# Sum of squared differences: several rows per load packet, float32 differences in place, a last row in five shrinking chunk pairs, and a seeded last sum

## The chip, the cores and the metric

The kernel runs on one core of a Trainium2 chip. The metric is the device time of one execution in microseconds (us). The profile's span is about 1.8 us shorter than that time. Runs of one kernel on one chip mostly agree within 0.3%; single runs lie further out.

## The reference

```python
batch, dim = 1024, 4096
x, y: float32 [1024, 4096]
out = np.sum((x - y) ** 2, axis=-1)        # float32 [1024]
```

The two inputs are 33.55 MB, the output 4 KB. Every element is read once, subtracted once and squared once.

## The kernel before

Partition p holds the rows 8p to 8p + 7, one of them per step i. VectorE subtracts into a bfloat16 tile, and ScalarE squares and sums it (its output goes to a dummy tile in PSUM, the sum to one column of `results`). The rows 6 and 7 are cut into chunks, so that work can begin before a whole row is there. Some chunks are squared on VectorE instead ("DD"), by an operation that multiplies and sums at once. In the trace that operation is CUSTOM_DVE_ANT_0 with a short READ_ACCUMULATOR after it.

```python
w6 = [2258, 1838];                 s6 = ["DA", "DD"]
w7 = [1467, 1316, 619, 308, 386];  s7 = ["DA", "DA", "DA", "DD", "DD"]

for i in range(ntiles - 2):                       # rows 0..5, data pool with 2 buffers
    xt, yt = data.tile([P, D], float32), data.tile([P, D], float32)
    dt = data.tile([P, D], bfloat16)
    nc.sync.dma_start(out=xt, in_=x[i:B:ntiles, :])
    nc.sync.dma_start(out=yt, in_=y[i:B:ntiles, :])
    nc.vector.tensor_sub(out=dt, in0=xt, in1=yt)
    nc.scalar.activation(out=junk, in_=dt, func=Square, accum_out=results[:, i : i + 1])
# ... loads of all chunks of rows 6 and 7 (cut) ...
emit_compute(w6, s6, ...)                         # per chunk: subtraction, then square-sum on ACT or DVE
nc.vector.tensor_reduce(out=results[:, i6 : i6 + 1], in_=part6, ...)
emit_compute(w7, s7, ...)
nc.vector.tensor_reduce(out=results[:, i7 : i7 + 1], in_=part7, ...)
nc.sync.dma_start(out=out, in_=results)
```

Of the kernel before, what the change touches and what calls it, by code (L numbers as in the profile page):

```python
# [1 line left out]
_os.environ.setdefault("NEURON_RT_ULTRASERVER_MODE", "4")  # L2

# [1 line left out]

# [4 lines left out]


@with_exitstack
def kernel(
    ctx: ExitStack,
    tc: tile.TileContext,
    x: bass.AP,
    y: bass.AP,
    axis: bass.AP,
    out: bass.AP,
):  # L20
    nc = tc.nc
    P = nc.NUM_PARTITIONS

    B, D = x.shape
    ntiles = (B + P - 1) // P

    data = ctx.enter_context(tc.tile_pool(name="data", bufs=2))
    chunkp = ctx.enter_context(tc.tile_pool(name="chunk", bufs=1))
    res = ctx.enter_context(tc.tile_pool(name="res", bufs=1))
    junkp = ctx.enter_context(tc.tile_pool(name="junkp", bufs=1, space=bass.MemoryType.PSUM))  # L30

    w6 = [2258, 1838]
    s6 = ["DA", "DD"]
    w7 = [1467, 1316, 619, 308, 386]
    s7 = ["DA", "DA", "DA", "DD", "DD"]
    assert sum(w6) == D and sum(w7) == D
    K6 = len(w6)
    K7 = len(w7)

    results = res.tile([P, ntiles], mybir.dt.float32)  # L40
    part6 = res.tile([P, K6], mybir.dt.float32)
    part7 = res.tile([P, K7], mybir.dt.float32)
    junk = junkp.tile([P, D], mybir.dt.float32)

    Square = mybir.ActivationFunctionType.Square
    i6 = ntiles - 2
    i7 = ntiles - 1

    xts = []
    yts = []  # L50
    dts = []
    for i in range(ntiles - 2):
        xt = data.tile([P, D], mybir.dt.float32, name="xt")
        yt = data.tile([P, D], mybir.dt.float32, name="yt")
        dt = data.tile([P, D], mybir.dt.bfloat16, name="dt")
        nc.sync.dma_start(out=xt, in_=x[i:B:ntiles, :])  # L56
        nc.sync.dma_start(out=yt, in_=y[i:B:ntiles, :])  # L57
        xts.append(xt)
        yts.append(yt)
        dts.append(dt)  # L60

        nc.vector.tensor_sub(out=dt, in0=xt, in1=yt)  # L62
        nc.scalar.activation(  # L63
            out=junk,
            in_=dt,
            func=Square,
            accum_out=results[:, i : i + 1],
        )

    def emit_chunks(tid, widths, strats, part):  # L70
        cxs, cys, cds, sqs = [], [], [], []
        c0 = 0
        for k, w in enumerate(widths):
            cx = chunkp.tile([P, w], mybir.dt.float32, name=f"cx{tid}_{k}")
            cy = chunkp.tile([P, w], mybir.dt.float32, name=f"cy{tid}_{k}")
            cd = chunkp.tile([P, w], mybir.dt.bfloat16, name=f"cd{tid}_{k}")
            nc.sync.dma_start(out=cx, in_=x[tid:B:ntiles, c0 : c0 + w])  # L77
            nc.sync.dma_start(out=cy, in_=y[tid:B:ntiles, c0 : c0 + w])
            sq = None
            if strats[k] == "DD":  # L80
                sq = chunkp.tile([P, w], mybir.dt.bfloat16, name=f"sq{tid}_{k}")
            cxs.append(cx)
            cys.append(cy)
            cds.append(cd)
            sqs.append(sq)
            c0 += w
        return cxs, cys, cds, sqs

    cx6, cy6, cd6, sq6 = emit_chunks(i6, w6, s6, part6)
    cx7, cy7, cd7, sq7 = emit_chunks(i7, w7, s7, part7)  # L90

    def emit_compute(widths, strats, cxs, cys, cds, sqs, part):
        for k, w in enumerate(widths):
            nc.vector.tensor_sub(out=cds[k], in0=cxs[k], in1=cys[k])  # L94
            if strats[k] == "DA":
                nc.scalar.activation(  # L96
                    out=junk[:, 0:w],
                    in_=cds[k],
                    func=Square,
                    accum_out=part[:, k : k + 1],  # L100
                )
            else:
                nc.vector.tensor_tensor_reduce(  # L103
                    out=sqs[k],
                    in0=cds[k],
                    in1=cds[k],
                    scale=1.0,
                    scalar=0.0,
                    op0=mybir.AluOpType.mult,
                    op1=mybir.AluOpType.add,  # L110
                    accum_out=part[:, k : k + 1],
                )

    emit_compute(w6, s6, cx6, cy6, cd6, sq6, part6)
    nc.vector.tensor_reduce(  # L115
        out=results[:, i6 : i6 + 1],
        in_=part6,
        axis=mybir.AxisListType.X,
        op=mybir.AluOpType.add,
    )  # L120
    emit_compute(w7, s7, cx7, cy7, cd7, sq7, part7)
    nc.vector.tensor_reduce(  # L122
        out=results[:, i7 : i7 + 1],
        in_=part7,
        axis=mybir.AxisListType.X,
        op=mybir.AluOpType.add,
    )

    nc.sync.dma_start(out=out, in_=results)


# [1 line left out]
_INS = ['x', 'y', 'axis']  # L133
_OUTS = [((1024,), 'float32')]
#: Inputs that are plain numbers.
_NUMBERS = {'axis': -1}


# [26 lines left out]
```

## Time and profile before

| what | before |
|---|---|
| time, median | 87.84 us (87.72 to 87.92) |
| span | 86.0 us |
| DMA packets | 3888 |
| one full pair of rows (4 MiB), landing to landing | 9.79 us, 428 GB/s |
| VectorE and ScalarE busy | 39.6 us and 29.4 us |
| store issued | 83.65 us |

VectorE and ScalarE are busy for less than half of the span, and the chain of waits on the page, shown in the prediction, is 78% DMA: the kernel waits for its loads. A read of the profile therefore splits into the start until the first bytes flow, the stream of loads, and the tail from the last landings to the store. (A load lands when its data are in; the wait for it ends then.) The span ends some 2.35 us after the store is issued.

### The profile page before, as it was taken

Reading aid. Unit: us, or ns where it says so; the run is one execution under the profiler, and the core shown is the slowest. Engines: PE = TensorE matmul, PEld = TensorE weight load, DVE = VectorE, ACT = ScalarE, POOL = GpSimd, SP = SyncE. Lnnn points to the kernel's source line nnn. Section 1 sums busy time; section 2 is a strip of 40 time slices with the busy share of each in tenths; the row PEclk is TensorE's granted clock in tenths of the full one; section 3 lists DMA queues with packets and bytes.
Section 4 is the critical chain, followed back from the end, with each engine's and each line's share of the span. In section 5 each row is a group of like instructions: output and inputs, shape, how many; then the busy total and the mean of one; then the engine's idle time right before and its main releaser. Section 6 shows DMA issues by size and latency. Waiting matters only on the chain.

```text
span 86.0 us, 143 instructions
## 1 busy us (share of the span) xinstructions
DVE 39.6 (46%) x21; ACT 29.4 (34%) x21; POOL 0.2 (0%) x4
## 2 busy tenths in 40 slices
DVE  0000009900496008910397007930198655996980
ACT  5000000098003940079002950069000996007630
POOL 0000000000000000000000000000000000000000
DMA  4799999999999999999999999999999999999900
GB/s 107 320 427 442 412 465 389 473 396 465 404 450 404 457 396 457 404 450 412 442 419 435 427 427 435 419 442 412 408 420 411 424 418 416 408 416 390 314 0 2
DMA packets 3888, 33.56 MB, mean 390 GB/s; under 512 B 560, under 2 KB 1072, under 8 KB 2096
## 3 DMA queue, kind: packets, MB, share of 16 engines
q1 hardware_dynamic: 3888, 33.56, 93.5%
HBM read 33.55 MB, written 0.00 MB: 390 GB/s over the span
## 4 chain that ended last, share of the span: by engine, by line
DMA 78%; DVE 14%; SPq 3%; issue 1%; DVEq 0%
DMA yt<-in_y_dram 41%; DMA cy<-in_y_dram 37%; DVE dt L62 10%; DVE cd L94 2%; SPq L56 2%; DVE sq L103 1%; SPq L57 1%; SPq L77 1%; DVE results L122 0%; DVEq L62 0%; DVEq L94 0%; DVEq L122 0%; DVE part L103 0%
## 5 line engine op out<-in xcount | busy, mean ns | idle before, releaser
L62 DVE TENSOR_TENSOR dt<-xt,yt 128x4096 bf16<-128x4096 f32 x6 | 26.6, 4425 | 39.8 <-DMA yt<-in_y_dram 39.8
L63 ACT ACTIVATE junk<-dt 128x4096 f32<-128x4096 bf16 x6 | 21.5, 3587 | 45.9 <-DVE dt L62 45.9
L94 DVE TENSOR_TENSOR cd<-cx,cy 128x2258 bf16<-128x2258 f32 (+6 forms) x7 | 9.7, 1379 | 3.9 <-DMA cy<-in_y_dram 3.8
L96 ACT ACTIVATE junk<-cd 128x2258 f32<-128x2258 bf16 (+3 forms) x4 | 5.4, 1354 | 6.5 <-DVE cd L94 6.4
L103 DVE CUSTOM_DVE_ANT_0 sq<-cd 128x1838 bf16<-128x1838 bf16 (+2 forms) x3 | 3.1, 1038 | 0.1
L63 ACT ACT_TABLE_LOAD x1 | 1.3, 1283 | 0.7 <-PEq L146 0.7
L63 ACT ACTIVATION_READ_ACCUMULATOR junk<-dt 128x1 f32 x6 | 1.1, 186 | 0.0
L96 ACT ACTIVATION_READ_ACCUMULATOR junk<-cd 128x1 f32 x4 | 0.7, 186 | 0.0
L103 DVE DVE_READ_ACCUMULATOR2_ANT part<- 128x1 f32 x3 | 0.2, 83 | 0.0
L122 DVE TENSOR_REDUCE results<-part 128x1 f32<-128x5 f32 x1 | 0.2, 159 | 0.1
L115 DVE TENSOR_REDUCE results<-part 128x1 f32<-128x2 f32 x1 | 0.2, 155 | 0.1
L146 POOL MEMSET const-bfloat16-1.0<- 128x1 bf16 x1 | 0.1, 102 | 0.0
L146 POOL MEMSET const-uint8-127<- 128x1 uint8 x1 | 0.1, 102 | 0.0
L146 POOL MEMSET const-float32-1.0<- 128x1 f32 x1 | 0.1, 99 | 0.0
L146 POOL MEMSET const-float32-0.0<- 128x1 f32 x1 | 0.1, 98 | 0.2 <-issue 0.2
## 6 DMA issues: line engine op xcount, KB each, us to landing
xt<-in_x_dram SPq DMA_DIRECT2D x6, 2048.0 KB, 10.1
yt<-in_y_dram SPq DMA_DIRECT2D x6, 2048.0 KB, 14.6
cx<-in_x_dram SPq DMA_DIRECT2D x1, 1129.0 KB, 16.9
cy<-in_y_dram SPq DMA_DIRECT2D x1, 1129.0 KB, 19.2
cx<-in_x_dram SPq DMA_DIRECT2D x1, 919.0 KB, 20.9
cy<-in_y_dram SPq DMA_DIRECT2D x1, 919.0 KB, 22.7
cx<-in_x_dram SPq DMA_DIRECT2D x1, 733.5 KB, 24.0
cy<-in_y_dram SPq DMA_DIRECT2D x1, 733.5 KB, 23.3
```

The lines of the kernel that those rows point to most:

```text
L56: nc.sync.dma_start(out=xt, in_=x[i:B:ntiles, :])
L57: nc.sync.dma_start(out=yt, in_=y[i:B:ntiles, :])
L62: nc.vector.tensor_sub(out=dt, in0=xt, in1=yt)
L63: nc.scalar.activation(out=junk, in_=dt, func=Square, accum_out=results[:, i : i + 1],)
L77: nc.sync.dma_start(out=cx, in_=x[tid:B:ntiles, c0 : c0 + w])
L94: nc.vector.tensor_sub(out=cds[k], in0=cxs[k], in1=cys[k])
L96: nc.scalar.activation(out=junk[:, 0:w], in_=cds[k], func=Square, accum_out=part[:, k : k + 1],)
L103: nc.vector.tensor_tensor_reduce(out=sqs[k], in0=cds[k], in1=cds[k], scale=1.0, scalar=0.0, op0=mybir.AluOpType.mult, op1=mybir.AluOpType.add,
L115: nc.vector.tensor_reduce(out=results[:, i6 : i6 + 1], in_=part6, axis=mybir.AxisListType.X, op=mybir.AluOpType.add,)
L122: nc.vector.tensor_reduce(out=results[:, i7 : i7 + 1], in_=part7, axis=mybir.AxisListType.X, op=mybir.AluOpType.add,)
L146: nc = _bacc.Bacc("TRN2", target_bir_lowering=False, num_devices=1)
```

## The change

Its intent is to spend fewer packets on the same bytes (a packet is the part of a load that goes to one partition; the trace has 128 of them per transfer and 16 more of 4 bytes, so 27 transfers make 3888): four rows of x in one load (64 KB per partition), then pairs of rows (32 KB). VectorE writes the float32 difference over x, so no tiles for differences are needed, and five large buffers fit: one of 64 KB per partition and four of 32 KB. Row 7 comes in five pairs that shrink. The last reduction is to move off the end: it runs before the last square-sum, and its result is the start value (the seed) of that sum. Row 6 is no longer cut.

```diff
-        nc.sync.dma_start(out=xt, in_=x[i:B:ntiles, :])         # per row, 16 KB per partition
-        nc.sync.dma_start(out=yt, in_=y[i:B:ntiles, :])
+    xv = x.rearrange("(p r) d -> p (r d)", p=P)
+    load(x03, xv, 0, 4 * D)                                     # 64 KB per partition
+    load(y01, yv, 0, 2 * D)                                     # 32 KB
+    load(y23, yv, 2 * D, 4 * D)
+    load(x45, xv, 4 * D, 6 * D)
+    load(y45, yv, 4 * D, 6 * D)
 ...
-        nc.vector.tensor_sub(out=dt, in0=xt, in1=yt)            # dt is bfloat16
+            nc.vector.tensor_sub(out=a, in0=a, in1=b)           # float32, over x
 ...
+    w7 = [1280, 1088, 768, 640, 320]
+    on_act = [True, False, True, True, False]
 ...
+        nc.vector.tensor_sub(out=a, in0=a, in1=b)
+        if k == K - 1:
+            nc.vector.tensor_reduce(out=head, in_=part, ...)    # parts 0..3
+        if on_act[k]:
+            square_sum(a, part[:, k : k + 1])
+        else:
+            nc.vector.tensor_tensor_reduce(
+                out=b, in0=a, in1=a, ...
+                scalar=head if k == K - 1 else 0.0,
+                accum_out=results[:, R - 1 : R] if k == K - 1 else part[:, k : k + 1],
+            )
```

More of the change, by code (lines that the diff above doesn't have):

```diff
@@ L22 @@
     P = nc.NUM_PARTITIONS
+    F32 = mybir.dt.float32
+    Square = mybir.ActivationFunctionType.Square
     B, D = x.shape
-    ntiles = (B + P - 1) // P
-    data = ctx.enter_context(tc.tile_pool(name="data", bufs=2))
-    chunkp = ctx.enter_context(tc.tile_pool(name="chunk", bufs=1))
+    R = B // P
+    xv = x.rearrange("(p r) d -> p (r d)", p=P)
+    yv = y.rearrange("(p r) d -> p (r d)", p=P)
+    ov = out.rearrange("(p r) -> p r", p=P)
+    wide = ctx.enter_context(tc.tile_pool(name="wide", bufs=1))
@@ L29 @@
+    pairs = ctx.enter_context(tc.tile_pool(name="pairs", bufs=1))
     res = ctx.enter_context(tc.tile_pool(name="res", bufs=1))
     junkp = ctx.enter_context(tc.tile_pool(name="junkp", bufs=1, space=bass.MemoryType.PSUM))
-    w6 = [2258, 1838]
-    s6 = ["DA", "DD"]
-    w7 = [1467, 1316, 619, 308, 386]
-    s7 = ["DA", "DA", "DA", "DD", "DD"]
-    assert sum(w6) == D and sum(w7) == D
-    K6 = len(w6)
-    K7 = len(w7)
-    results = res.tile([P, ntiles], mybir.dt.float32)
-    part6 = res.tile([P, K6], mybir.dt.float32)
@@ L42 @@
-    part7 = res.tile([P, K7], mybir.dt.float32)
-    junk = junkp.tile([P, D], mybir.dt.float32)
-    Square = mybir.ActivationFunctionType.Square
-    i6 = ntiles - 2
-    i7 = ntiles - 1
-    xts = []
-    yts = []
-    dts = []
-    for i in range(ntiles - 2):
-        xt = data.tile([P, D], mybir.dt.float32, name="xt")
-        yt = data.tile([P, D], mybir.dt.float32, name="yt")
-        dt = data.tile([P, D], mybir.dt.bfloat16, name="dt")
-        nc.sync.dma_start(out=xt, in_=x[i:B:ntiles, :])
-        nc.sync.dma_start(out=yt, in_=y[i:B:ntiles, :])
-        xts.append(xt)
-        yts.append(yt)
-        dts.append(dt)
-        nc.vector.tensor_sub(out=dt, in0=xt, in1=yt)
+    results = res.tile([P, R], F32)
@@ L63, with load, square_sum @@
+    junk = junkp.tile([P, D], F32)
+    w7 = [1280, 1088, 768, 640, 320]
+    on_act = [True, False, True, True, False]
+    assert sum(w7) == D
+    K = len(w7)
+    part = res.tile([P, K - 1], F32)
+    head = res.tile([P, 1], F32)
+    def load(dst, src, c0, c1):
+        nc.sync.dma_start(out=dst, in_=src[:, c0:c1])
+    def square_sum(d, acc):
         nc.scalar.activation(
-            out=junk,
-            in_=dt,
-            func=Square,
-            accum_out=results[:, i : i + 1],
-        )
@@ L70, in emit_chunks @@
-    def emit_chunks(tid, widths, strats, part):
-        cxs, cys, cds, sqs = [], [], [], []
-        c0 = 0
-        for k, w in enumerate(widths):
-            cx = chunkp.tile([P, w], mybir.dt.float32, name=f"cx{tid}_{k}")
-            cy = chunkp.tile([P, w], mybir.dt.float32, name=f"cy{tid}_{k}")
-            cd = chunkp.tile([P, w], mybir.dt.bfloat16, name=f"cd{tid}_{k}")
-            nc.sync.dma_start(out=cx, in_=x[tid:B:ntiles, c0 : c0 + w])
-            nc.sync.dma_start(out=cy, in_=y[tid:B:ntiles, c0 : c0 + w])
-            sq = None
-            if strats[k] == "DD":
-                sq = chunkp.tile([P, w], mybir.dt.bfloat16, name=f"sq{tid}_{k}")
-            cxs.append(cx)
-            cys.append(cy)
-            cds.append(cd)
-            sqs.append(sq)
-            c0 += w
-        return cxs, cys, cds, sqs
@@ L89 @@
-    cx6, cy6, cd6, sq6 = emit_chunks(i6, w6, s6, part6)
-    cx7, cy7, cd7, sq7 = emit_chunks(i7, w7, s7, part7)
-    def emit_compute(widths, strats, cxs, cys, cds, sqs, part):
-        for k, w in enumerate(widths):
-            nc.vector.tensor_sub(out=cds[k], in0=cxs[k], in1=cys[k])
-            if strats[k] == "DA":
-                nc.scalar.activation(
-                    out=junk[:, 0:w],
-                    in_=cds[k],
-                    func=Square,
-                    accum_out=part[:, k : k + 1],
-                )
-            else:
-                nc.vector.tensor_tensor_reduce(
-                    out=sqs[k],
-                    in0=cds[k],
-                    in1=cds[k],
-                    scale=1.0,
-                    scalar=0.0,
-                    op0=mybir.AluOpType.mult,
-                    op1=mybir.AluOpType.add,
-                    accum_out=part[:, k : k + 1],
-                )
@@ L114 @@
-    emit_compute(w6, s6, cx6, cy6, cd6, sq6, part6)
-    nc.vector.tensor_reduce(
-        out=results[:, i6 : i6 + 1],
-        in_=part6,
-        axis=mybir.AxisListType.X,
-        op=mybir.AluOpType.add,
-    )
-    emit_compute(w7, s7, cx7, cy7, cd7, sq7, part7)
-    nc.vector.tensor_reduce(
-        out=results[:, i7 : i7 + 1],
-        in_=part7,
-        axis=mybir.AxisListType.X,
-        op=mybir.AluOpType.add,
-    )
-    nc.sync.dma_start(out=out, in_=results)
+            out=junk[:, 0 : d.shape[1]], in_=d, func=Square, accum_out=acc
+        )
@@ new lines, in rows @@
+    def rows(xt, yt, n, r0):
+        for k in range(n):
+            a = xt[:, k * D : (k + 1) * D]
+            b = yt[:, k * D : (k + 1) * D]
+            nc.vector.tensor_sub(out=a, in0=a, in1=b)
+            square_sum(a, results[:, r0 + k : r0 + k + 1])
+    x03 = wide.tile([P, 4 * D], F32, name="wide_x", tag="wide_x")
+    y01 = pairs.tile([P, 2 * D], F32, name="ya", tag="ya")
+    y23 = pairs.tile([P, 2 * D], F32, name="yb", tag="yb")
+    x45 = pairs.tile([P, 2 * D], F32, name="xc", tag="xc")
@@ new lines @@
+    y45 = pairs.tile([P, 2 * D], F32, name="yc", tag="yc")
+    load(x03, xv, 0, 4 * D)
[3 more added lines that the diff above has]
+    load(y45, yv, 4 * D, 6 * D)
+    rows(x03[:, 0 : 2 * D], y01, 2, 0)
+    rows(x03[:, 2 * D : 4 * D], y23, 2, 2)
+    t6 = pairs.tile([P, 2 * D], F32, name="ya2", tag="ya")
+    t7 = pairs.tile([P, 2 * D], F32, name="yb2", tag="yb")
+    load(t6[:, 0:D], xv, 6 * D, 7 * D)
+    load(t6[:, D : 2 * D], yv, 6 * D, 7 * D)
@@ new lines @@
+    c0 = 0
+    for w in w7:
+        load(t7[:, c0 : c0 + w], xv, 7 * D + c0, 7 * D + c0 + w)
+        load(t7[:, D + c0 : D + c0 + w], yv, 7 * D + c0, 7 * D + c0 + w)
+        c0 += w
+    rows(x45, y45, 2, 4)
+    rows(t6[:, 0:D], t6[:, D : 2 * D], 1, 6)
+    c0 = 0
+    for k, w in enumerate(w7):
+        a = t7[:, c0 : c0 + w]
+        b = t7[:, D + c0 : D + c0 + w]
+        nc.vector.tensor_sub(out=a, in0=a, in1=b)
+        if k == K - 1:
+            nc.vector.tensor_reduce(
+                out=head, in_=part, axis=mybir.AxisListType.X, op=mybir.AluOpType.add
+            )
[3 more added lines that the diff above has]
+            nc.vector.tensor_tensor_reduce(
+                out=b,
+                in0=a,
+                in1=a,
+                scale=1.0,
+                scalar=head if k == K - 1 else 0.0,
+                op0=mybir.AluOpType.mult,
+                op1=mybir.AluOpType.add,
+                accum_out=results[:, R - 1 : R] if k == K - 1 else part[:, k : k + 1],
+            )
+        c0 += w
@@ L133 @@
+    nc.sync.dma_start(out=ov, in_=results)
 _INS = ['x', 'y', 'axis']
```

## The prediction

> **What bounds the kernel now.** I read the page first: the 40 slices and the DMA queue, then the chain of waits, to see whether transfers or engines set the pace.
>
> ```profile
> DVE  0000009900496008910397007930198655996980
> DMA  4799999999999999999999999999999999999900
> GB/s 107 320 427 442 412 465 389 473 396 465 404 450 404 457 396 457 404 450 412 442 419 435 427 427 435 419 442 412 408 420 411 424 418 416 408 416 390 314 0 2
> q1 hardware_dynamic: 3888, 33.56, 93.5%
> DMA 78%; DVE 14%; SPq 3%; issue 1%; DVEq 0%
> ```
>
> The DMA row is full from the third slice to the 38th, and the chain is 78% DMA. VectorE is busy only until the last eight slices, where it is dense. So there are three terms: a start (slices 1 and 2 lack traffic), a stream without holes, and a tail in which VectorE works close behind the last loads. The stages in windows (window, length, busy time of VectorE, ScalarE and GpSimd, clock, DMA share, GB/s), cut at the landings of the pairs, show the stream's rate:
>
> ```profile
> 12.84:22.63 9.79, 4.43 (x1) 3.71 (x2) 0.00 (x0) 1.00 1.02 435
> 42.23:52.01 9.78, 4.42 (x1) 3.71 (x2) 0.00 (x0) 1.00 1.01 429
> 71.73:82.10 10.37, 9.16 (x9) 3.89 (x7) 0.00 (x0) 1.00 0.95 371
> ```
>
> A pair of full rows (4 MiB) takes 9.79 us, 428 GB/s; per pair VectorE works 4.4 us and ScalarE 3.7 us, so they idle more than half of the time. In the last window VectorE is busy 9.16 of 10.37 us. The timeline shows the end (start, length, engine, line, operation):
>
> ```profile
> 81.71 0.48 DVE L103 CUSTOM_DVE_ANT_0 sq<-cd 128x308 bf16<-128x308 bf16 x1
> 82.19 0.56 DVE L94 TENSOR_TENSOR cd<-cx,cy 128x386 bf16<-128x386 f32 x1
> 82.78 0.56 DVE L103 CUSTOM_DVE_ANT_0 sq<-cd 128x386 bf16<-128x386 bf16 x1
> 83.46 0.16 DVE L122 TENSOR_REDUCE results<-part 128x1 f32<-128x5 f32 x1
> 83.65 0.35 SPq L129 DMA_DIRECT2D out_dram<-results  x1
> ```
>
> The last load is issued at 75.37 and lands 6.7 us later (DMA view), at 82.07. The store is issued at 83.65, lands in 1.4 us, and the span ends at 86.0: 2.35 us from store to end, which the change leaves alone.
>
> [...] The trace has only bfloat16: 3587 ns at 4096 and 1397 at 1467 give 0.833; float32 is not shown here. [...]
>
> **The change, part by part.** (a) **Packets.** 3888 packets are 27 transfers of 144: 128 rows and 16 completions. The new kernel has 17 loads (5 big, 2 of one row, 10 chunks) and the store, 18 x 144 = 2592. What is a packet worth? One engine of the 16 carries 262,144 bytes and 18 packets per pair in 9.795 us. From 61.81 (landing of pair 5) to 82.07 it carries 524,288 bytes in 14 loads x 9 = 126 packets in 20.27 us. Twice the first is 19.59 us with 36 packets; so 90 more packets cost 0.68 us, **7.6 ns each** (estimate), and the bytes alone run at 262,144 / (9.795 - 0.137) = 27.14 B/ns, 434 GB/s over 16. The stream goes from 234 packets per engine to 153: 81 x 7.6 ns = **0.6 us** less in all. Up to the sixth row it is 108 against 45 packets, 0.48 us: rows 4 and 5 should be in at 61.81 - 0.48 = 61.3, row 6 at 61.3 + 9.8 = 71.1. The chunk pairs carry 16 x width x 4 bytes and 18 packets per engine: 1280 takes 3.15 us, 1088 2.7, 768 1.95, 640 1.65, 320 0.9, so they land at about 74.3, 77.0, 78.9, 80.6 and 81.5.
>
> (b) **Early stages.** Nothing can be computed until 12 MiB are in, at about 32 us, instead of 12.9. It costs nothing by itself: four subtractions of 4.43 us end at about 51 (two after each pair of rows of y), before rows 4 and 5 are in. Row 6 reuses the first y buffer, free at 41; the chunks reuse the second, free at 51; the queue then still holds ten microseconds and more of data. So the stream should have no hole.
>
> (c) **Tail on VectorE.** Here lies the cost. Row 6 is no longer cut (before 2258 + 1838); its 4096-wide subtraction starts at 71.24 (0.1 after landing, as in the trace) and ends at 75.67. All later loads but none keep VectorE waiting after that. Subtractions and float32 square-sums by (N + 152) / 0.96 ns, which fits the trace's 2510, 1691, 561; gaps as in the trace, 0.08 before a new load's consumer, 0.02 before a square-sum: 1280 ends 77.23; 1088 at 78.60; its square-sum, 1.29, at 79.92; 768 at 80.88; 640 at 81.78; 320 at 82.35.
>
> (d) **Tail on ScalarE.** By 0.833 N + 175 ns, 0.12 for the accumulator read and 0.04 to 0.09 for hand-over: row 6 from 75.77 to 79.48, 1280 to 80.88, 768 to 81.91, 640 to 82.77. So ScalarE is just behind VectorE, and the reduction of the four parts starts at 82.86 instead of right after the last subtraction.
>
> (e) **Seeded sum.** The reduction (0.16) now stands before the last square-sum, not after it: 83.02; hand-over 0.09; square-sum of 320, 0.49; store issued at **83.64**. Before: 83.65. The reorder saves nothing if it waits for ScalarE: its 0.16 us still lies on the path. What (a) gives, 0.5 us at row 6, the uncut row 6 and the backlog take back. Bare sum: a span of 86.0, **87.85 us**.
>
> I move this down a little for the start. In quarter-microsecond windows, the first 16 packets, one per engine, are counted at 1.5 to 2.5 us, the next wave at 2.75 to 3.25, and the following ones 0.6 us apart. So some 0.6 us is lost after each engine's first 16 KB. If that is the time until its next packet is ready, a first packet of 64 KB covers it and every later time moves up by 0.6. I give that about even odds: 0.3 us, hence **87.5 us**.
>
> **Rivals.** First, **large packets gain more**: the start's 0.6 us in full[...]. For it: the hole at the start. Against: at 428 of 434 little is left, and the tail is VectorE's. [...] Third, **a hole in the stream**: the sync queue stands still for a buffer (first y buffer until 41, second until 51). [...] Against: 10 to 20 us of data are queued behind it. It would add its own length; I give it one in twenty. Fourth, **hidden anyway**: all gain of the stream is swallowed by the tail, 87.9 to 88.1.
>
> **Range and chances.** The bare sum 87.85 with the start gives 87.25 to 87.85[...]. Eight in ten: 86.5 to 88.7. For faster by 2% (below 86.1) 1.76 us must go, so both the start's hole and the whole packet overhead must be gained and nothing lost in the tail: 0.08. Slower by 2% (above 89.6)[...]: 0.05. Same: 0.87.
>
> **What would show it.** 2592 packets; windows between landings of the big loads at 431 to 434 GB/s; first subtraction near 32 us; rows 4 and 5 at 61.3 or, with the start's gain, 60.7; VectorE without a gap over 0.1 us from row 6's landing to the reduction, which waits for ScalarE; a float32 square-sum of 1088 at 1.29 us[...]; float32 activation of 4096 at 3.59 us; the store 12.4 us after row 6 landed. The prediction is wrong if the GB/s row dips in the middle, if row 6 lands after 71.5, or if the store follows row 6 by under 11.5 or over 13 us.

(N + 152) / 0.96 ns is a fit to VectorE's durations in the trace (4425 ns for 4096 elements is another of them), and that float32 square-sums follow it too was an estimate. A count "per engine" is a sixteenth of all packets; the records name no engine.

## The result, and the profile after

The changed kernel takes 87.75 us (median, 87.71 to 87.81) against 87.84 us: the same. The ratio is 0.9993, with a 95% interval of 0.9978 to 1.0007. When the changed kernel was run again later (after_same_chip), the ratio was 1.0003.

These are the 40 slices, the queue and the chain of waits from the changed kernel's page, in the same order as those of the kernel before:

```profile
DVE  0000000000000009999599960000399968999950
DMA  9099999759998999889997999889899989999600
GB/s 488 0 488 488 488 488 488 305 244 427 488 473 351 396 488 488 381 381 457 488 473 335 412 488 488 381 381 457 381 465 389 465 359 414 414 404 396 216 0 2
q1 hardware_dynamic: 2592, 33.56, 92.6%
DMA 71%; DVE 16%; ACT 5%; issue 3%; SPq 1%; ACTq 0%; DVEq 0%
```

The packets are 2592, as counted. The GB/s row swings between 0 and 488 because a packet is counted whole in the slice where it begins: 488 GB/s in a slice of 2.15 us is 1049 KB, just 16 packets of 64 KB or 32 of 32 KB. VectorE now starts at 32 us, and ScalarE is on the chain with 5%. That is new: in the last microseconds something waits for ScalarE.

The windows (window, length, busy time of VectorE, ScalarE and GpSimd, clock, DMA share, GB/s) are cut at landings of big loads:

```profile
32.29:61.45 29.16, 17.52 (x4) 14.84 (x8) 0.00 (x0) 1.00 1.00 430
61.45:71.25 9.80, 8.76 (x2) 4.58 (x3) 0.00 (x0) 1.00 0.98 416
```

In the first window land 12 MiB: 12,582,912 bytes in 29.16 us, or 431.5 GB/s. (The column says 430, because it counts whole packets in the window.) Before, the same bytes took three pairs of 9.79 us, 0.21 us more. The first 12 MiB were in at 32.29 instead of 32.44. Together, rows 4 and 5 are in at 61.45 instead of 61.81, 0.36 us earlier. Row 6 then takes 9.80 us, like a full pair before, and is in at 71.25; the two chunks of the kernel before were in at 71.73.

The end of the timeline (start, length, engine, line, operation; an idle time before it and what ended it in brackets):

```profile
79.75 2.31 DVE L96 TENSOR_TENSOR yb<-yb 128x768 f32<-128x768 f32 x3
...
81.98 0.71 ACT L53 ACTIVATE junk<-yb 128x640 f32<-128x640 f32 x1
82.62 0.19 ACT L53 ACTIVATION_READ_ACCUMULATOR junk<-yb 128x1 f32 x1
82.84 0.16 DVE L98 TENSOR_REDUCE head<-part 128x1 f32<-128x4 f32 x1 [0.78 <-ACT junk L53]
83.03 0.55 DVE L104 CUSTOM_DVE_ANT_0 yb<-yb,head 128x320 f32<-128x320 f32 x1
83.51 0.08 DVE L104 DVE_READ_ACCUMULATOR2_ANT results<- 128x1 f32 x1
83.66 0.35 SPq L116 DMA_DIRECT2D out_dram<-results  x1
```

VectorE ends its last subtraction at 82.06 and then stands for 0.78 us, until ScalarE has summed the 640-wide chunk. Only then come the reduction and, after it, 0.55 us of square-sum that could have run in the wait. The store goes out at 83.66 against 83.65 before. What the stream gained, 0.36 us at rows 4 and 5 and 0.48 at row 6, is gone by then.

### The profile page after: what moved, and what is told of

Same layout as the page of the kernel before. It is cut to its first block, busy times and chain, and to the rows that moved or that the text cites. A ratio compares the mean times of both kernels' runs of the same rounds, so it can differ in the third digit from the quotient of the medians.

```text
span 86.0 us, 123 instructions
## 1 busy us (share of the span) xinstructions
DVE 37.5 (44%) x17; ACT 30.4 (35%) x21; POOL 0.2 (0%) x4
## 2 busy tenths in 40 slices
DMA packets 2592, 33.56 MB, mean 390 GB/s; under 512 B 416, under 2 KB 672, under 8 KB 1696
## 3 DMA queue, kind: packets, MB, share of 16 engines
q1 hardware_dynamic: 2592, 33.56, 92.6%
## 4 chain that ended last, share of the span: by engine, by line
DMA 71%; DVE 16%; ACT 5%; issue 3%; SPq 1%; ACTq 0%; DVEq 0%
DMA ya<-in_y_dram 71%; DVE wide_x L61 10%; ACT junk L53 5%; DVE ya L61 5%; SPq L50 1%; DVE yb L104 1%; DVE head L98 0%; ACTq L147 0%; DVEq L61 0%; ACTq L53 0%; DVEq L147 0%
## 5 line engine op out<-in xcount | busy, mean ns | idle before, releaser
L61 DVE TENSOR_TENSOR wide_x<-wide_x,ya 128x4096 f32<-128x4096 f32 x2 | 8.8, 4422 | 32.4 <-DMA ya<-in_y_dram 32.4
L53 ACT ACTIVATE junk<-wide_x 128x4096 f32<-128x4096 f32 x4 | 14.3, 3588 | 15.8 <-DVE wide_x L61 15.8
L61 DVE TENSOR_TENSOR xc<-xc,yc 128x4096 f32<-128x4096 f32 x2 | 8.8, 4422 | 10.7 <-DMA yc<-in_y_dram 10.7
L53 ACT ACTIVATE junk<-xc 128x4096 f32<-128x4096 f32 x2 | 7.2, 3588 | 12.1 <-issue 11.4
L61 DVE TENSOR_TENSOR wide_x<-wide_x,yb 128x4096 f32<-128x4096 f32 x2 | 8.8, 4422 | 0.9 <-DMA yb<-in_y_dram 0.9
L96 DVE TENSOR_TENSOR yb<-yb 128x1280 f32<-128x1280 f32 (+4 forms) x5 | 5.0, 1010 | 0.1
L61 DVE TENSOR_TENSOR ya<-ya 128x4096 f32<-128x4096 f32 x1 | 4.4, 4426 | 1.1 <-DMA ya<-in_y_dram 1.1
L53 ACT ACTIVATE junk<-ya 128x4096 f32<-128x4096 f32 x1 | 3.6, 3588 | 1.8 <-DVE ya L61 1.8
L53 ACT ACTIVATE junk<-yb 128x1280 f32<-128x1280 f32 (+2 forms) x3 | 2.8, 921 | 0.1
L104 DVE CUSTOM_DVE_ANT_0 yb<-yb 128x1088 f32<-128x1088 f32 x1 | 1.3, 1291 | 0.0
```

The lines of the kernel that those rows point to most:

```text
L53: nc.scalar.activation(out=junk[:, 0 : d.shape[1]], in_=d, func=Square, accum_out=acc)
L61: nc.vector.tensor_sub(out=a, in0=a, in1=b)
L96: nc.vector.tensor_sub(out=a, in0=a, in1=b)
L104: nc.vector.tensor_tensor_reduce(out=b, in0=a, in1=a, scale=1.0, scalar=head if k == K - 1 else 0.0, op0=mybir.AluOpType.mult, op1=mybir.A ...
```

## The experiments

Twelve runs were made, in three groups. Those of one group ran on one chip, beside the kernel before: e1_seed_off to e4, then after_same_chip to e6, then e8 to e1_third.

### e1_seed_off: the changed kernel without the seed

```diff
-        if k == K - 1:
-            nc.vector.tensor_reduce(out=head, in_=part, ...)
...
-                scalar=head if k == K - 1 else 0.0,
-                accum_out=results[:, R - 1 : R] if k == K - 1 else part[:, k : k + 1],
+                scalar=0.0,
+                accum_out=part[:, k : k + 1],
...
+    nc.vector.tensor_reduce(out=results[:, R - 1 : R], in_=part, ...)   # five parts, at the end
```

> The changed kernel with the last reduction put back behind the last square-sum, as it was before (five parts, no seed). Theory: in the changed kernel VectorE is done with its last subtraction at 82.06, then stands 0.78 us until ScalarE delivers the fourth part at about 82.8, reduces (0.16) and only then runs the 320-wide square-sum (0.55). Without the seed the square-sum fits into that wait; the reduction still starts at about 82.85 and the store is issued near 83.05 instead of 83.66: 0.6 us faster, 87.15 (87.0 to 87.3). Rival (the seed does what it is meant for, takes 0.16 us and a hand-over off the end): 0.15 to 0.25 us slower, 87.95. Second rival (VectorE alone bounds the tail, its work is the same): unchanged, 87.75.

Measured: 87.05 us, ratio to before 0.9925 (0.9903 to 0.9947). The end of its timeline:

```profile
82.03 0.71 ACT L52 ACTIVATE junk<-yb 128x640 f32<-128x640 f32 x1
82.16 0.49 DVE L99 CUSTOM_DVE_ANT_0 yb<-yb 128x320 f32<-128x320 f32 x1
...
82.89 0.16 DVE L110 TENSOR_REDUCE results<-part 128x1 f32<-128x5 f32 x1 [0.24 <-ACT junk L52]
83.08 0.35 SPq L114 DMA_DIRECT2D out_dram<-results  x1
```

The square-sum now lies beside ScalarE's last activation. The reduction starts at nearly the same time as in the changed kernel (82.89 against 82.84), and VectorE's wait shrinks from 0.78 to 0.24 us. The store is 0.58 us earlier. The theory held, and both rivals fell.

### after_same_chip and e1_again: both on one chip

> The changed kernel itself, once more, so that it stands on the same chip as the next three. Both theories: ratio to before 0.998 to 1.001, store issued at 83.66 within 0.1.

> The changed kernel without the seed, again, now beside the changed kernel on one chip. If the seed costs what the first run said, it is 0.6 us faster than the changed kernel (0.5 to 0.8) and the reduction again starts 0.1 us after ScalarE's last accumulator read. If the first run's difference was one of chips, under 0.2 us.

The changed kernel took 87.85 us, ratio 1.0003 (0.9988 to 1.0018), with the store at 83.70. Without the seed it took 87.17 us, ratio 0.9932 (0.9914 to 0.995), with the store at 83.09. The difference of 0.7 us in time and 0.61 us at the store is no matter of chips.

### e5_seed_in_before and e8_seed_in_before_ordered: the seed alone

e8 is the kernel before with this change (e5 is the same without the `issue_after` line):

```diff
-    emit_compute(w7, s7, cx7, cy7, cd7, sq7, part7)
-    nc.vector.tensor_reduce(out=results[:, i7 : i7 + 1], in_=part7, ...)
+    emit_compute(w7[:-1], s7[:-1], cx7, cy7, cd7, sq7, part7)
+    last_sub = nc.vector.tensor_sub(out=cd7[-1], in0=cx7[-1], in1=cy7[-1])
+    with tc.issue_after(last_sub.ins):
+        nc.vector.tensor_reduce(out=head, in_=part7[:, 0 : K7 - 1], ...)
+    nc.vector.tensor_tensor_reduce(out=sq7[-1], in0=cd7[-1], in1=cd7[-1], ...
+        scalar=head, accum_out=results[:, i7 : i7 + 1])
```

> The kernel before with nothing but the seeded last sum (reduction of four parts ahead of the last square-sum of 386, its result as the seed). Theory: the seed costs only what it waits for ScalarE. Here ScalarE's last part is done at 82.54, before VectorE ends its last subtraction at 82.75, so there is no wait; the order of two instructions is swapped, the hand-over shrinks from 0.1 to 0.03 us and the square-sum with a seed is 0.06 us longer: store within 0.1 us of 83.65, time within 0.15 us of before. Rival (a seeded square-sum is itself dear, with the wait a side effect): 0.4 to 0.6 us slower. Rival (the seed does take the reduction off the end here, 0.16 us and a hand-over): 0.2 us or more faster.

e5 took 88.11 us, ratio 1.0037 (1.0024 to 1.0051). The 0.33 us lie between what the theory said (within 0.15) and the first rival (0.4 to 0.6). Its timeline shows why it doesn't count for that rival. The framework's scheduler had put the reduction ahead of the last subtraction, with a wait of its own:

```profile
82.54 0.16 DVE L124 TENSOR_REDUCE head<-part 128x1 f32<-128x4 f32 x1 [0.40 <-ACT junk L97]
82.62 0.56 DVE L123 TENSOR_TENSOR cd<-cx,cy 128x386 bf16<-128x386 f32 x1
```

> The kernel before with the seeded last sum again, this time with the reduction tied behind the last subtraction (in e5_seed_in_before the scheduler had moved it ahead of that subtraction, where VectorE stood 0.40 us waiting for ScalarE; that run mixed two things). Theory: ScalarE's last part is there at 82.5, before the last subtraction ends at 82.75, so no wait; reduction 82.78 to 82.94, seeded square-sum from 82.97, store 0.69 us after that (as in e5_seed_in_before) at 83.66: unchanged within 0.1 us, ratio 0.999 to 1.001. Rival (a seeded square-sum is dear by itself): 0.3 us or more slower even without the wait. Rival (it saves the reduction): 0.2 us or more faster.

With the order held, it took 87.78 us, ratio 0.9998 (0.9981 to 1.0014):

```profile
82.24 0.56 DVE L123 TENSOR_TENSOR cd<-cx,cy 128x386 bf16<-128x386 f32 x1
82.42 0.19 ACT L97 ACTIVATION_READ_ACCUMULATOR junk<-cd 128x1 f32 x1
82.72 0.15 DVE L125 TENSOR_REDUCE head<-part 128x1 f32<-128x4 f32 x1
82.91 0.62 DVE L131 CUSTOM_DVE_ANT_0 sq<-cd,head 128x386 bf16<-128x386 bf16 x1
...
83.60 0.35 SPq L142 DMA_DIRECT2D out_dram<-results  x1
```

Here the reduction has no wait in brackets, and the seed neither costs nor saves anything beyond 0.1 us: the store is 0.05 us earlier than in the kernel before, 0.10 if counted from the start of the last subtraction (82.24 against 82.19). The seeded square-sum of 386 takes 621 ns against 561 unseeded (for 320 elements, 552 ns in the changed kernel against 0.49 us in e1_seed_off), which eats most of what the shorter hand-over gives. So the seed is not dear by itself. In the changed kernel its price is the wait for ScalarE that it puts in front of the last square-sum. Between them, e5 and e8 repeat the pattern in another kernel: with a wait for ScalarE it is slower, without one it is equal.

### e2_one_row_loads: the packets alone

```diff
-    load(x03, xv, 0, 4 * D)
-    load(y01, yv, 0, 2 * D)
-    ...
+    for t, v, r0, n in ((x03, xv, 0, 4), (y01, yv, 0, 2), (y23, yv, 2, 2), (x45, xv, 4, 2), (y45, yv, 4, 2)):
+        for k in range(n):
+            load(t[:, k * D : (k + 1) * D], v, (r0 + k) * D, (r0 + k + 1) * D)
```

> The changed kernel with rows 0 to 5 loaded one row per transfer (16 KB packets), in the same order into the same tiles; all else the same. Theory (7.6 ns per packet, and the tail follows row 6): 108 packets per engine instead of 45 before row 6, 0.4 to 0.5 us later; row 6 lands at about 71.7 instead of 71.25, the store goes out 0.4 us later, 88.15. If the start with 64 KB packets is itself later by 0.07 us, 0.35 us. Rival (packet size buys nothing here[...]): 87.75. Rival (the first packet's hole of 0.6 us depends on its size): more than 0.6 us either way.

Measured: 88.02 us, ratio 1.0031 (1.0012 to 1.0051). The changed kernel's ratios were 0.9993 and 1.0003 in other sessions, so the big packets are worth 0.28 to 0.38%, some 0.3 us. Row 6's subtraction starts at 71.64 against 71.36, and the store goes out at 83.93 against 83.66. The rival that packets buy nothing fell. The later the row lands, the later the store, one for one.

Over 63 packets per engine, 0.28 us would be 4.4 ns each, short of the fit of 7.6. But this average mixes two stages. These are the subtractions that wait for the first 12 MiB and for the first 24 MiB, in e2 and then in the changed kernel:

```profile
32.45 4.42 DVE L61 TENSOR_TENSOR wide_x<-wide_x,ya 128x4096 f32<-128x4096 f32 x1 [0.46 <-DMA ya<-in_y_dram]
61.82 4.43 DVE L61 TENSOR_TENSOR xc<-xc,yc 128x4096 f32<-128x4096 f32 x1 [0.47 <-DMA yc<-in_y_dram]
```

```profile
32.39 8.76 DVE L61 TENSOR_TENSOR wide_x<-wide_x,ya 128x4096 f32<-128x4096 f32 x2 [32.39 <-DMA ya<-in_y_dram]
61.53 8.76 DVE L61 TENSOR_TENSOR xc<-xc,yc 128x4096 f32<-128x4096 f32 x2 [10.73 <-DMA yc<-in_y_dram]
```

The second 12 MiB take 29.37 us in e2, as in the kernel before (32.54 to 61.91), and 29.14 in the changed kernel (29.13 in e1_seed_off, which has its loads and ran on the chip of e2). So 27 packets cost 0.23 us, 8.5 ns each, a little more than the fit. Up to the first 12 MiB the changed kernel has 36 packets fewer, worth 0.3 us at that price, but it is only 0.06 us ahead. Some 0.2 us is lost in the start with 64 KB packets (estimate, from these numbers). The third rival looked in the right place, but the effect is smaller than its 0.6 us.

### e3_before_float32: the type alone

```diff
-        dt = data.tile([P, D], mybir.dt.bfloat16, name="dt")
+        dt = data.tile([P, D], mybir.dt.float32, name="dt")
         ... likewise cd and sq
```

> The kernel before with every bfloat16 difference and square made float32, in tiles of its own as they were, so no wait for a buffer changes. Theory[...]: the same, 87.84 within 0.1, 4096-wide subtraction 4.42 us and activation 3.59 us, fused square-sum of 1838 at 2.07.[...]

Measured: 87.86 us, ratio 1.0017 (0.9997 to 1.0038). From the groups of instructions by form (busy us, mean ns):

```profile
L62 DVE TENSOR_TENSOR dt<-xt,yt 128x4096 f32<-128x4096 f32 x6 | 26.5, 4425 | 39.8 <-DMA yt<-in_y_dram 39.8
L63 ACT ACTIVATE junk<-dt 128x4096 f32<-128x4096 f32 x6 | 21.5, 3587 | 45.9 <-DVE dt L62 45.9
L103 DVE CUSTOM_DVE_ANT_0 sq<-cd 128x1838 f32<-128x1838 f32 x1 | 2.1, 2074 | 0.0
```

In the kernel before, with bfloat16, the same three took 4425, 3587 and 2074 ns. The theory held: here the type is neutral in time, also for the square-sum, which has one tile as both sources.

### e4_big_loads_old_tail: big loads with the tail of before

The edit: the changed kernel up to row 5. Then row 6 is loaded and worked as 2258 + 1838 and row 7 as 1467, 1316, 619, 308, 386, on the engines and with the reductions of the kernel before, in float32 and in place.

> The changed kernel's big loads of rows 0 to 5 with the tail of before behind them (row 6 as 2258 + 1838, row 7 as 1467, 1316, 619, 308, 386, same engines, reductions at the end; float32 in place). Theory: the stream is 0.36 us earlier at row 6 as in the changed kernel, but rows 4 and 5 arrive together at 61.45, so VectorE is busy with them until 70.3 and starts on the first half of row 6 three microseconds after it landed; the backlog carries to the end and the store goes out at 83.65 to 83.9, 87.75 to 88.0. Rival (the old tail keeps its distance to the landings and the packets' gain comes through): 87.4 to 87.5.

Measured: 87.51 us, ratio 0.9981 (0.9956 to 1.0006), with the store at 83.24. The theory fell and its rival is nearer. VectorE did begin row 6 late, at 70.15, and the backlog did reach row 7. The last line is from the kernel before:

```profile
76.85 0.16 DVE L103 TENSOR_REDUCE results<-part 128x1 f32<-128x2 f32 x1
76.96 4.24 DVE L93 TENSOR_TENSOR yb<-yb 128x1467 f32<-128x1467 f32 x4
81.23 0.48 DVE L97 CUSTOM_DVE_ANT_0 yb<-yb 128x308 f32<-128x308 f32 x1
```

```profile
78.69 2.99 DVE L94 TENSOR_TENSOR cd<-cx,cy 128x1316 bf16<-128x1316 f32 x3 [0.77 <-DMA cy<-in_y_dram]
```

Row 7 begins 0.73 us later than in the kernel before (76.96 against 76.23). But there VectorE stood 0.77 us for the second chunk's landing, until 78.69. Here it runs four subtractions through in 4.24 us, although their own durations add up to 4.48: each of the last three starts some 0.08 us before the one ahead of it ends. The fifth operation, the square-sum of 308, starts at 81.23 instead of 81.71. The slack took up the backlog, and the packets' gain came through: the store is 0.41 us earlier than before. In time this is a fifth of a per cent, and the interval includes 1, so a gain in time is not shown.

### e6_tail_refit: a first try at a better version

The edit to e1: row 6 in two chunks with a reduction of its own in the middle of the tail, and row 7 in six chunks.

> A try at a better version: the changed kernel's big loads, no seed, row 6 in two chunks (2304, 1792, both squared on ScalarE, their sum taken in the middle of the tail), row 7 in six chunks (1856, 1024, 352, 416, 288, 160; the third and the last squared on VectorE). Widths from a small model of landings and engine times that puts the stores of the runs without the seed and with the old tail within 0.05 us. It says store at 82.8, 0.25 us before the version without the seed: 0.8 to 0.9 us under before. Rival (short chunks cost the stream more than the model's 6.5 ns per packet, or hand-overs between the engines eat it): the same as without the seed or slower.

Measured: 89.12 us, ratio 1.0149 (1.0134 to 1.0163), the slowest of all. As in e5, the scheduler had moved the reduction forward, ahead of row 7, where VectorE stood for ScalarE:

```profile
78.17 0.15 DVE L120 TENSOR_REDUCE results<-part 128x1 f32<-128x2 f32 x1 [3.50 <-ACT junk L54]
78.28 3.66 DVE L105 TENSOR_TENSOR yb<-yb 128x1856 f32<-128x1856 f32 x3
```

The run says nothing about its widths, and the model's 6.5 ns per packet is below the 8.5 that e2 showed. It says once more what one reduction costs that waits for ScalarE in front of other work: 3.5 us of VectorE.

### e9_tail_refit_ordered, e7_four_pairs and e1_third

e9, on e1's base: row 6 as 2304 + 1792, row 7 as 1984, 1056, 416, 448, 192, the sums of both rows in one zeroed tile, and a single reduction at the end for both. e7, on e1's base: only the line of widths.

```diff
-    w7 = [1280, 1088, 768, 640, 320]
-    on_act = [True, False, True, True, False]
+    w7 = [2080, 832, 800, 384]
+    on_act = [True, False, True, False]
```

> The try at a better version again, without the reduction in the middle that the scheduler of e6_tail_refit had moved ahead of row 7 (VectorE stood 3.5 us there): both rows' parts lie in one tile with zeros in the unused places and one reduction at the end sums both. Row 6 as 2304 + 1792 on ScalarE, row 7 in five chunks 1984, 1056, 416, 448, 192, the third and the last squared on VectorE. Model: store at 82.8, 0.25 to 0.3 us before the version without the seed, ratio 0.989 to 0.992. Rival (row 6 whole or cut, the end is set by the last landings and hand-overs): within 0.1 us of the version without the seed.

> The version without the seed with row 7 in four pairs (2080, 832, 800, 384; the second and the last squared on VectorE) and row 6 whole. Model: store at 82.9, 0.1 to 0.15 us before five pairs; 18 packets per engine fewer. Rival (a last chunk of 384 instead of 320 means more work after the last landing): 0.1 us slower than five pairs.

> The version without the seed, to stand on the same chip as these. Ratio to before 0.992 to 0.994, store at 83.08 within 0.1.

Measured, all on one chip beside before at 87.83 us:

| kernel | median us | ratio to before | 95% interval |
|---|---|---|---|
| e7, four pairs | 86.96 | 0.9904 | 0.9879 to 0.9928 |
| e9, row 6 cut, five pairs | 86.96 | 0.9904 | 0.9884 to 0.9924 |
| e1, only the seed undone | 87.13 | 0.9927 | 0.9901 to 0.9954 |

All three beat both kernels. Four pairs or a cut row 6 may add 0.2 us, but the intervals overlap, so that is not settled. The profiles of e7 and e9 fell on the longest of their runs (87.43 and 87.34 us). Their stores, at 83.43 and 83.12, are later than the 82.8 to 82.9 of the model and than the 82.92 of e1_third, and can't be taken for the typical run, so the model is neither confirmed nor refuted.

## Why the prediction was right

It said the same, 87.5 us, with a range of 86.5 to 88.7, and 87.75 was measured. By its own steps:

- **Packets (a).** The count of 2592 is exact. The gain up to rows 4 and 5 was put at 0.48 us and measured 0.36 between the two kernels, and 0.29 when packets alone were changed (e2). By the last load the stream is about 0.6 us ahead, as said (issued at 74.40 and 7.1 us to landing, against 75.37 and 6.7). The mechanism is right, and so is the price, 8.5 ns by e2 against 7.6. What is missing from the 0.48 was lost in the start, below.
- **No hole, late first work (b).** The first subtraction came at 32.39 ("about 32"), and rows 4 and 5 at 61.45 ("61.3"). Row 6 landed at 71.25 ("71.1"), 9.80 us later, at the same pace as before. No hole showed. Read to the letter, its sign "the GB/s row dips in the middle" came true (335 at slice 22), but that is the counting of whole packets; the landings show no hole. One of its readings is garbled, too: VectorE isn't "busy only until the last eight slices", but mostly idle until then.
- **VectorE's tail (c).** The float32 square-sum of 1088 took 1291 ns ("1.29"), and VectorE had no gap over 0.1 us until the reduction. Its end was mis-sized: 82.06 instead of 82.35, as the 0.08 us put in front of each subtraction did not show. ScalarE, which was later, hid that. The store came 12.41 us after row 6 had landed ("12.4").
- **ScalarE and the seed (d, e).** ScalarE's last part set the reduction at 82.84 ("82.86"), the store followed at 83.66 ("83.64"), and "its 0.16 us still lies on the path" held. That the store was met to 0.02 us is partly luck: row 6 landed some 0.1 us later than the sum had it, and the way from there to the reduction was as much shorter. The prediction stopped short here. It saw the wait and called the reorder worthless, but didn't see that it was harmful: without it the square-sum fits into the wait, and 0.6 us are saved (e1, twice repeated).
- **Who took the gain back.** The prediction named "the uncut row 6 and the backlog". The runs say otherwise. By the stores of the profiles, big loads with the old tail come to 83.24 (e4), 0.41 earlier than before. The new widths with row 6 uncut but no seed come to 83.08, another 0.16 earlier. The seed brings it back to 83.66, 0.58 later. So the big loads and the new chunks (widths and uncut row together; row 6 uncut alone was not run) both gain, and the seed takes the gain back. It does so only with this tail: the wait it meets is ScalarE working off the uncut row 6 and three parts without a pause from 75.88 on, and in the kernel before the seed costs nothing (e8). In time, e1 is 0.46 us faster than e4 on the same chip, not 0.16; the rest comes after the store is issued, and no run settles why.
- **The start: the one mechanism that failed.** "If that is the time until its next packet is ready, a first packet of 64 KB covers it" is wrong, and with it the 0.3 us taken off the bare sum of 87.85, which was the better number. In quarter-microsecond windows (last columns DMA share and GB/s), first of the kernel before, then of the changed one, packets show up in waves:

```profile
1.75:2.00 0.25, 0.00 (x0) 0.25 (x1) 0.00 (x0) 1.00 3.01 655
3.00:3.25 0.25, 0.00 (x0) 0.00 (x0) 0.00 (x0) 1.00 1.68 721
```

```profile
1.75:2.00 0.25, 0.00 (x0) 0.00 (x0) 0.00 (x0) 1.00 8.88 2884
5.00:5.25 0.25, 0.00 (x0) 0.00 (x0) 0.00 (x0) 1.00 4.84 2097
```

A DMA share of 8.88 is more than 16 engines can do in that window, so a packet is counted where it begins, with its whole duration. That gives the duration of one. 2884 GB/s in 0.25 us are 11 packets of 64 KB, and 8.88 x 0.25 us x 16 engines are 35.5 us: 3.23 us each. In the second wave it is 2.42 us, so a packet of the first wave takes 0.8 us longer. With 16 KB it is 1.20 us against 0.61, 0.6 longer. The loss belongs to the first 16 packets (one per engine, if they are dealt evenly), and larger ones do not cover it. It varies: by the traces' packet records, the first 16 packets took on average 0.58 to 0.79 us longer than later ones in the nine profiles with 64 KB (3204 against 2419 ns in the changed kernel), and 0.50 to 0.63 in the five with 16 KB (1110 against 613 ns in the kernel before). The larger packet tends to lose more, which fits the 0.2 us that e2 found missing in the start. Why, no run shows.

## What to carry to other kernels

Taking an instruction off the end can help only if what it needs is ready when it moves forward, and even then e8 gained no more than 0.1 us. A reduction that waits for another engine belongs behind all work that could run in that wait (e1: 0.58 us at the store), and the idle time in brackets before it shows which case it is. Compare the instruction order on each engine with the source before judging a run: twice here a scheduler moved a small reduction in front of other work, and the run measured that instead of the edit. When loads set the pace, each packet saved was worth about 8.5 ns per engine once the stream ran, but opening it with 64 KB packets lost some 0.2 us of that (estimate from e2). A small first load before the large ones was not tried. Any gain then has to pass the tail, so follow it there, landing by landing.
